# A hybrid SSD and gated-MLP layer: state products in three float32r parts, and the decay matrix made in place from rows loaded by direction

## The chip, the core and the metric

The kernel runs on one core of a Trainium2 chip, as one program in one launch. The metric is the device time of one execution in microseconds (us), first to last instruction plus what lies around them. TensorE is PE in the profile, VectorE DVE, ScalarE ACT, GpSimd POOL, and SyncE, which issues most loads, SP.

## What is computed

One layer of a trunk works on 256 latent tokens that read a prefix of 256 context tokens; the width is 2048. One input projection feeds a Mamba-2 state-space part (SSD; 32 heads of 64 in 8 groups, state size 128, two chunks of 128 tokens, both directions) and a gating MLP. All is float32. The part that matters here, for one direction:

```python
xbc = silu(dwconv_rows(z[..., :XBC_W], conv_w, conv_b))       # x, B and C of all groups
acs = cumsum(dt * A, axis=2)                                  # per chunk
decay_to_end = exp(a_tot[:, :, None] - acs)
states = einsum('bckgn,bckgr,bckgrp->bcgrpn', Bc, decay_to_end, xdt)
...
CB    = einsum('bcqgn,bckgn->bcgqk', Cc, Bc)
Lmat  = exp(where(mask, acs_t[..., :, None] - acs_t[..., None, :], -inf))
y_diag = einsum('bcgqk,bcgrqk,bckgrp->bcqgrp', CB, Lmat, xdt)
y_off  = einsum('bcqgn,bcgrpn,bcqgr->bcqgrp', Cc, h_starts, exp(acs))
y = y_diag + y_off                                            # then gates, norms, output projection
```

The context tokens only make the states from which the latent scans of both directions start.

## The kernel before, in words

**Projection.** The 4096 columns of x, B and C are done in 32 tiles of 128 columns. A group g has four: tiles 4g and 4g+1 (x), 4g+2 (B) and 4g+3 (C, latent tokens alone, so 256 wide in place of 512). A float32 product of nearly full precision is made of three products of float32r parts. ACT casts a weight half to its high part, DVE subtracts that from the raw half for the low part (`hi_w`, `lo_w`, lines 542 and 548, 128x1024 each), and `mm3` (lines 140 to 142) issues high by high, low by high and high by low for each of 16 pieces of the contraction. So a tile of 512 is 48 matmuls into one PSUM bank, `psx`; the tiles take turns between two such banks. Tiles 0 to 3, 12, 13 and 15 are made earlier; 12, 13 and 15 wait in SBUF (`y`, `zq`).

**After its products** a tile goes through ACT (line 607, middle tap and bias: `xbc<-psx,pc`), DVE (line 623, the other taps of the convolution, which read the PSUM bank as well: 8 instructions, 4 for a tile of 256) and ACT (line 626, silu). Its bank is free after the last tap. x and B are also turned to have tokens on partitions, by DVE and two DMAs (`tx`, `Dx`, `xk`; `tb`, `Db`, `bk`).

**The SSD of a group.** The names in the profile are: `xw` (POOL, line 785), x times dt times the decay to the end, for the states of the context; `psc`, the product of it with B over two tiles of context tokens (line 868, plain float32); `xl` and `psl`, the same for the latent tokens; `hs`, the states at the start of each chunk (ACT copies `psc`, POOL and DVE add the rest, lines 878 to 890); `pcb`, `cbb` and `cbf`, C by B and its two triangles; `M` (POOL line 896, DVE line 904), C by B times dt in both directions; `pso`, C by `hs` (plain float32); `psy`, the product of the decayed M with x; `yo`, `yc`, `yz` and `pty`, the outputs on their way into `y`.

**The decay matrix.** The cumulated logarithms lie in a DRAM scratch `acs`. For each group one POOL DMA copies its 2048 values to all partitions (`R`, 1 MB, line 724). ACT adds a column to each of its 16 blocks of 128x128 (line 820, `ssd_d`), DVE takes the minimum of the two directions into another tile `E` (line 827, two instructions), ACT takes the exponential of all of it (line 833), with a table load ahead of it and one behind it for the next silu, and DVE multiplies M into E (line 906). `R` has one buffer; the load for the next group waits for the second minimum.

**What sets the order.** Each engine runs its instructions in the order of the code. That order comes from a queue: `later(dt, fn)` puts a step at a due time on a clock that the loop over the projection's pieces drives, 1.3 for each two pieces (0.65 in a tile of 256), and `pump` issues what is due. `plan_tile` gives every step its offset from the end of its tile. `late` moves the whole second part of a group (from `ssd_cb` on), and `td` its end:

```python
for t, fn in [(6, ssd_cb), (6, ssd_states), ..., (12, ssd_o), ..., (16 + td, ssd_yd), (16.9 + td, ssd_yc), ...]:
    later(d0 + t, lambda fn=fn: fn(g))
plan_d(d0 + 11, g + 1, 1.5)      # the next group's decay matrix: four calls of ssd_d,
plan_e(d0 + 17, g + 1)           # then the minima and the exponential
```

`cv1`, `cv2` and `cv3` are pools of one, two and three buffers for each tag.

## Time and profile before

| what | value |
|---|---|
| median of three runs | 962.25 us (961.64 to 963.29) |
| the profiled execution | 962.39 us, its span 960.6 us, clock granted to PE 0.998 |
| busy in the span: PE, DVE, ACT, POOL | 950.8, 675.0, 481.8, 192.1 us |
| psc of a group (line 868), 8 groups | 4 records each, 15.3 us in all, 596 ns each |
| decay rows: blocks (820), minima (827), exponentials (833) | 128, 16 and 8 instructions |

Starts are in us from the start of the span. A plain float32 matmul leaves two records in the profile. Rows on PE overlap, since matmuls are pipelined: the time that one holds PE is the distance to the next start, not the length shown. DVE and ACT rows overlap by less than 0.1 us.

### The profile page before, as it was taken

To read this page: it belongs to the slowest core of one execution; us is meant where nothing else is said; L and a number is where in the kernel's file an instruction comes from. 1 tells how busy PE (TensorE), PEld (TensorE's weight loads), DVE (VectorE), ACT (ScalarE), POOL (GpSimd) and SP (SyncE) were. 2 spreads that over 40 slices of the span, in tenths; PEclk is the share of its full clock that TensorE was granted. 3 is DMA by queue.
4 is the path that set the end of the run, shared out by engine and by line. 5 is a ranking of instruction groups with operands and counts; after the bars stand their busy time and mean duration, and the time that the engine had idled before them with its cause. 6 is when DMAs were issued, how large, how long until landed. Compare 5 with 4: busy or idle time off the path is not lost.

```text
span 960.6 us, 13754 instructions
## 1 busy us (share of the span) xinstructions
PE 950.8 (99%) x5128; PEld 769.6 (80%) x5128; DVE 675.0 (70%) x1108; ACT 481.8 (50%) x728; POOL 192.1 (20%) x294
## 2 busy tenths in 40 slices
PE   9999999999999999999999999999999999999997
PEld 4688888778787878787888888888888888888885
DVE  6888899889787776676766776766666665445636
ACT  4344358565564544455445443455665554355522
POOL 0000002423424324243000000043445440000000
PEclk9999999999999999999999999999999999999999
DMA  9999967468668667467787777786666666556722
GB/s 366 418 415 416 365 232 203 124 167 190 168 148 224 146 205 160 143 180 258 296 304 283 261 275 294 269 304 215 220 219 211 228 211 215 186 190 243 267 88 87
DMA packets 149970, 225.63 MB, mean 235 GB/s; under 512 B 119296, under 2 KB 119552, under 8 KB 127248
## 3 DMA queue, kind: packets, MB, share of 16 engines
q1 hardware_dynamic: 142992, 207.08, 64.0%
q0 software_dynamic: 6336, 16.86, 5.3%
q8 instruction: 40, 0.66, 0.3%
q10 hardware_dynamic: 576, 0.82, 0.2%
q14 instruction: 26, 0.21, 0.1%
HBM read 211.29 MB, written 9.25 MB: 230 GB/s over the span
## 4 chain that ended last, share of the span: by engine, by line
PE 93%; DVE 3%; DMA 2%; issue 1%; POOL 1%; ACT 0%; SPq 0%; POOLq 0%; ACTq 0%
PE pa L1192 12%; PE pa L1191 12%; PE pa L1193 12%; PE psx L140 9%; PE psx L142 9%; PE psx L141 9%; PE pm L1232 3%; PE pm L1233 3%; PE pm L1234 3%; PE pq L1234 2%; PE pq L1232 2%; PE pq L1233 2%; PE psada L253 2%; DMA ada<-in_wada_dram 1%; PE pso L920 1%; PE psc L868 1%
## 5 line engine op out<-in xcount | busy, mean ns | idle before, releaser
L87 DVE TENSOR_TENSOR lo_w<-w,hi_w 128x1024 fp32r<-128x1024 f32 x173 | 209.8, 1221 | 133.8 <-ACT hi_w L86 133.7
L86 ACT CAST hi_w<-w 128x1024 fp32r<-128x1024 f32 x173 | 181.9, 1053 | 206.4 <-PE pa L1193 138.1
L1191 PE MATMUL pa<-hi_w,hhi 128*128 128x512 f32 x512 | 200.5, 392 | 0.0
L1193 PE MATMUL pa<-hi_w,hlo 128*128 128x512 f32 x512 | 199.3, 389 | 0.0
L1192 PE MATMUL pa<-lo_w,hhi 128*128 128x512 f32 x512 | 199.2, 389 | 0.0
L140 PE MATMUL psx<-hhi,hi_w 128*128 128x512 f32 (+1 forms) x400 | 151.3, 378 | 1.0 <-DVE xbc L623 1.0
L142 PE MATMUL psx<-hhi,lo_w 128*128 128x512 f32 (+1 forms) x400 | 145.6, 364 | 0.0
L141 PE MATMUL psx<-hlo,hi_w 128*128 128x512 f32 (+1 forms) x400 | 145.6, 364 | 0.0
L1191 PEld LDWEIGHTS pa<-hi_w,hhi 128*128 128x128 f32 x512 | 96.1, 188 | 20.2 <-issue 0.4
L1193 PEld LDWEIGHTS pa<-hi_w,hlo 128*128 128x128 f32 x512 | 96.1, 188 | 20.0
L1192 PEld LDWEIGHTS pa<-lo_w,hhi 128*128 128x128 f32 x512 | 96.1, 188 | 19.9 <-issue 0.2
L548 DVE TENSOR_TENSOR lo_w<-w,hi_w 128x1024 fp32r<-128x1024 f32 x61 | 76.9, 1268 | 17.1 <-ACT hi_w L542 17.0
L623 DVE SCALAR_TENSOR_TENSOR xbc<-psx,pc,xbc 128x248 f32<-128x248 f32 (+1 forms) x204 | 83.3, 471 | 7.7 <-ACT xbc L607 6.9
L140 PEld LDWEIGHTS psx<-hhi,hi_w 128*128 128x128 f32 x400 | 75.4, 189 | 15.5 <-issue 3.1
L141 PEld LDWEIGHTS psx<-hlo,hi_w 128*128 128x128 f32 x400 | 75.5, 189 | 13.0 <-issue 1.7
L542 ACT CAST hi_w<-w 128x1024 fp32r<-128x1024 f32 x61 | 63.4, 1043 | 44.6 <-PE psx L141 30.8
L142 PEld LDWEIGHTS psx<-hhi,lo_w 128*128 128x128 f32 x400 | 75.4, 189 | 12.2
L1232 PE MATMUL pm<-hi_w,hhi 128*128 128x512 f32 x128 | 49.8, 389 | 0.0
L1233 PE MATMUL pm<-lo_w,hhi 128*128 128x512 f32 x128 | 49.8, 389 | 0.0
L1234 PE MATMUL pm<-hi_w,hlo 128*128 128x512 f32 x128 | 49.8, 389 | 0.0
L1071 DVE SCALAR_TENSOR_TENSOR junk<-gate,cb 128x2048 bf16<-128x2048 f32 x16 | 36.6, 2291 | 18.4 <-DMA gate<-in_wada_dram 18.4
L1096 POOL DMA_DIRECT2D y<-T x64 | 36.9, 584 | 47.6 <-ACT sq L1167 32.6
(268 smaller groups left out, 1405.7 us busy)
## 6 DMA issues: line engine op xcount, KB each, us to landing
w<-in_wlat_dram SPq DMA_DIRECT2D x64, 1024.0 KB, 4.9
w<-in_wout_dram SPq DMA_DIRECT2D x32, 1024.0 KB, 4.8
w<-in_wxbc_dram SPq DMA_DIRECT2D x25, 1024.0 KB, 6.6
ada<-in_wada_dram SPq DMA_DIRECT2D x24, 1024.0 KB, 13.7
gate<-in_wada_dram SPq DMA_DIRECT2D x16, 1024.0 KB, 5.4
ada<-in_wada_dram SPq DMA_DIRECT2D x16, 512.0 KB, 12.4
R<-acs POOLq DMA_DIRECT2D x8, 1024.0 KB, 7.2
wst<-in_wst_dram SPq DMA_DIRECT2D x15, 480.0 KB, 12.9
```

The costliest lines, as they stand in the source:

```text
L86: nc.scalar.copy(hi, raw)
L87: nc.vector.tensor_tensor(lo, raw, hi.bitcast(F32), op=ALU.subtract)
L140: nc.tensor.matmul(ps, lhsT=whi, rhs=hhi[k][:, s], start=start, stop=False)
L141: nc.tensor.matmul(ps, lhsT=whi, rhs=hlo[k][:, s], start=False, stop=False)
L142: nc.tensor.matmul(ps, lhsT=wlo, rhs=hhi[k][:, s], start=False, stop=stop)
L623: nc.vector.scalar_tensor_tensor(ao, zi, cw[:, k : k + 1], ao, op0=ALU.mult, op1=ALU.add)
L1191: nc.tensor.matmul(pa[tk], lhsT=hhi[k][:, t], rhs=whi[:, w], start=k == 0, stop=False)
L1192: nc.tensor.matmul(pa[tk], lhsT=hhi[k][:, t], rhs=wlo[:, w], start=False, stop=False)
L1193: nc.tensor.matmul(pa[tk], lhsT=hlo[k][:, t], rhs=whi[:, w], start=False, stop=k == KT - 1)
L1232: nc.tensor.matmul(p, lhsT=yh[:, t], rhs=whi[:, w], start=j == 0, stop=False)
L1233: nc.tensor.matmul(p, lhsT=yh[:, t], rhs=wlo[:, w], start=False, stop=False)
L1234: nc.tensor.matmul(p, lhsT=yl[:, t], rhs=whi[:, w], start=False, stop=hf == 0 and j == 15)
```

## The change

**State products.** For groups 1 to 6 both operands of `psc` are split, as the weights are. `ssd_w` writes x's share for each of the two context tiles apart (`xr`, POOL). `ssd_wp` casts each to its high part (`xwh`, ACT, 128x512) and subtracts (`xwl`, DVE, 128x512); `ssd_bp` does so with B (`bp`, ACT and DVE, 128x256). `ssd_states` then issues three float32r matmuls for each tile, six for a group, in place of two plain ones. Groups 0 and 7 keep their plain products. `pso` stays as it was (`out_parts` is false for every group, so `ssd_cp` and `ssd_hp` are never called).

**Decay rows.** `R` becomes two tiles, `R1` and `R0`, one for each direction, each loaded on its own (512 KB). The minimum is written over `R0`, and exponential and M's product stay there, so there is no `E`. Hence `R1` of the next group waits for the minima of this one as before, but `R0` for `psy` of this group. ACT's blocks of `R1` keep their place (`d0 + 11`); those of `R0` move to `d0 + 24 + td`, 1.0 apart, and minima and exponential from `d0 + 17` to `d0 + 28.5 + td`.

**Places.** `late` is 18 in place of 14 for group 1 and 20 in place of 17 for group 3; some other steps of these groups move by 1.5 to 7.5.

```diff
-    acs = drp.tile([32, 4 * P], F32, name="acs")
+    acs = drp.tile([2, 32, 2 * P], F32, name="acs")
...
-    def row_load(g):
+    def row_load(g, d):
...
-        R = cv1.tile([P, 4, 2, 2, P], F32, tag="R", name=f"R{g}")
-        nc.gpsimd.dma_start(R.rearrange("p h d c q -> p (h d c q)"),
-                            acs[4 * g : 4 * g + 4, :].rearrange("h x -> (h x)").unsqueeze(0).partition_broadcast(P))
-        rows_[g] = R
+        R = cv1.tile([P, 4, 2, P], F32, tag=f"R{d}", name=f"R{d}_{g}")
+        nc.gpsimd.dma_start(R.rearrange("p h c q -> p (h c q)"),
+                            acs[d, 4 * g : 4 * g + 4, :].rearrange("h x -> (h x)").unsqueeze(0).partition_broadcast(P))
+        rows_[g, d] = R
...
+    def out_parts(g):
+        return False
+
+    def state_parts(g):
+        return 0 < g < NGRP - 1
...
+            if t is not None:
+                S["xr", t] = cv2.tile([P, 2, 256], F32, tag="tt", name=f"xr{g}{t}")
...
+    def hi_lo(hi, lo, raw):
+        nc.scalar.copy(hi, raw)
+        nc.vector.tensor_tensor(lo, raw, hi.bitcast(F32), op=ALU.subtract)
+
+    def pair4(g, nm):
+        return [cv1.tile([P, 2, 2, 256], F32R, tag=f"{w}p", name=f"{nm}{w}{g}") for w in "hl"]
+
+    def ssd_wp(g, t):
+        S = gs_[g]
+        if t == 0:
+            S["xp"] = pair4(g, "xw")
+        hi_lo(S["xp"][0][:, t], S["xp"][1][:, t], S["xr", t])
+
+    def ssd_bp(g):
+        S = gs_[g]
+        bp = S["bp"] = cv1.tile([P, 2, 2, P], F32R, tag="yo1", name=f"bp{g}")
+        hi_lo(bp[:, 0], bp[:, 1], S["bk"][:, 0:2])
...
     def ssd_min(g, c):
-        R = rows_[g]
-        if c == 0:
-            gs_.setdefault(g, {})["E"] = cv1.tile([P, 2, 4, P], F32, tag="E", name=f"E{g}")
-        nc.vector.tensor_tensor(gs_[g]["E"][:, c], R[:, :, 0, c, :], R[:, :, 1, c, :], op=ALU.min)
+        R = rows_[g, 0]
+        gs_.setdefault(g, {})["E"] = R
+        nc.vector.tensor_tensor(R[:, :, c, :], R[:, :, c, :], rows_[g, 1][:, :, c, :], op=ALU.min)
         if c == 1:
-            later(12 if g == 4 else 0, lambda: row_load(g + 1))
+            later(LATER_B.get(g, 0), lambda: row_load(g + 1, 1))
...
         for t in range(2):
-            nc.tensor.matmul(psc, lhsT=bk[:, t, :], rhs=xw[:, t], start=t == 0, stop=t == 1)
+            if state_parts(g):
+                bh, bl = (S["bp"][:, i, t] for i in range(2))
+                xh, xo = (p[:, t] for p in S["xp"])
+                nc.tensor.matmul(psc, lhsT=bh, rhs=xh, start=t == 0, stop=False)
+                nc.tensor.matmul(psc, lhsT=bh, rhs=xo, start=False, stop=False)
+                nc.tensor.matmul(psc, lhsT=bl, rhs=xh, start=False, stop=t == 1)
+            else:
+                nc.tensor.matmul(psc, lhsT=bk[:, t, :], rhs=S["xw"][:, t], start=t == 0, stop=t == 1)
...
-            late = max(late, 17.0 if i == 15 else 14.0)
+            late = max(late, {7: 18.0, 15: 20.0}.get(i, 14.0))
...
+            if state_parts(g):
+                WS = 1.5 * (g == 3)
+                for t in range(2):
+                    later(d0 + tx + tw + 1.3 * t + WS, lambda t=t: ssd_w(g, t))
+                    later(d0 + tx + tw + WP + 1.5 * t + WS, lambda t=t: ssd_wp(g, t))
+            else:
+                later(d0 + tx + tw, lambda: ssd_w(g))
...
+                later(d0 + tx + BP + 7.5 * (g == 3), lambda: ssd_bp(g))
...
+                          (16 + td, ssd_yd), (16.9 + td, ssd_yc), (17.2 + td, lambda g: row_load(g + 1, 0)),
...
-            plan_d(d0 + 11, g + 1, 1.5)
-            plan_e(d0 + 17, g + 1)
+            plan_d(d0 + 11, g + 1, 1.5, 1)
+            plan_d(d0 + 24 + td, g + 1, 1.0, 0)
+            plan_e(d0 + 28.5 + td, g + 1)
+
+    WP, BP, TP = 3.0, 14.5, 8.0
```

**What stands where, at group 1.** On PE, the products of group 1's second part stood right behind tile 9 and ahead of the first product of tile 10 (`psx10`) before:

```order
L142 MATMUL psx9_2049<-hhi15_131,lo_w11_1934 128x512
L851 MATMUL pcb1_2149<-xbc7_1911,xbc6_1830 128x128 x2
L868 MATMUL psc1_2152<-xw1_1981,bk1_1953 128x512 x2
L871 MATMUL psl1_2155<-xl1_2024,bk1_1953 128x256 x2
L140 MATMUL psx10_2158<-hhi0_116,hi_w12_1979 128x512
```

Now they stand behind 18 of the 48 products of tile 10:

```order
L142 MATMUL psx10_2155<-hhi5_121,lo_w12_1996 128x512
L890 MATMUL pcb1_2196<-xbc7_1913,xbc6_1832 128x128 x2
L910 MATMUL psc1_2199<-xwh1_2023,bp1_2140 128x512
L911 MATMUL psc1_2199<-xwl1_2024,bp1_2140 128x512
L912 MATMUL psc1_2199<-xwh1_2023,bp1_2140 128x512
L910 MATMUL psc1_2199<-xwh1_2023,bp1_2140 128x512
L911 MATMUL psc1_2199<-xwl1_2024,bp1_2140 128x512
L912 MATMUL psc1_2199<-xwh1_2023,bp1_2140 128x512
L917 MATMUL psl1_2206<-xl1_2075,bk1_1955 128x256 x2
L140 MATMUL psx10_2155<-hhi6_122,hi_w12_1981 128x512
```

Two plain products became six, and the whole block moved 18 matmuls back; the same holds for `pso1` behind it.

On ACT, the exponential of group 1's decay matrix (`E1`) stood between the copy of group 0's `psy` and the silu of tile 8:

```order
L954 COPY yc0_2079<-psy0_2060 128x512
L833 ACT_TABLE_LOAD
L833 ACTIVATE E1_2081<-E1_2081 128x1024
L626 ACT_TABLE_LOAD
L626 ACTIVATE xbc8_2056<-xbc8_2056 128x512
L542 CAST hi_w14_2122<-w7_1868 128x1024
L607 ACTIVATE xbc9_2165<-psx9_2049,pc_87 128x512
L542 CAST hi_w15_2167<-w7_1868 128x1024
L878 COPY hs1_2187<-psc1_2152 128x2x256
L820 ACTIVATE R2_2092<-R2_2092,y_68 128x128 x4
L626 ACTIVATE xbc9_2165<-xbc9_2165 128x512
L542 CAST hi_w16_2237<-w8_1977 128x1024
```

Now it stands one tile later, between tile 9's first pass over its bank and the copy of `psc1` to `hs1`, with the cast of B and the blocks of `R0` ahead of it:

```order
L542 CAST hi_w14_2119<-w7_1870 128x1024
L800 CAST bp1_2140<-bk1_1955 128x256
L858 ACTIVATE R0_1_2088<-R0_1_2088,y_68 128x128 x6
L607 ACTIVATE xbc9_2162<-psx9_2047,pc_87 128x512
L542 CAST hi_w15_2164<-w7_1870 128x1024
L858 ACTIVATE R0_1_2088<-R0_1_2088,y_68 128x128 x2
L870 ACT_TABLE_LOAD
L870 ACTIVATE R0_1_2088<-R0_1_2088 128x1024
L626 ACT_TABLE_LOAD
L626 ACTIVATE xbc9_2162<-xbc9_2162 128x512
L924 COPY hs1_2231<-psc1_2199 128x2x256
L542 CAST hi_w16_2235<-w8_1979 128x1024
```

The silu of tile 9, the copy to `hs1` and the cast of `hi_w16` now come behind the exponential of this group.

On DVE, behind the taps of the stored tile 12, the minima of group 2 stood ahead of the taps of tile 10, and M's products of group 1 had been issued before these rows:

```order
L623 SCALAR_TENSOR_TENSOR xbc12_2248<-y_68,pc_87,xbc12_2248 128x254
L738 STREAM_TRANSPOSE tx21_2266<-xbc9_2165 128x4x4x32
L926 TENSOR_TENSOR yo10_2270<-pso10_2231,ed_1460 128x512
L926 TENSOR_TENSOR yo11_2276<-pso11_2232,ed_1460 128x512
L738 STREAM_TRANSPOSE yc1_2307<-psy1_2298 128x4x4x32
L827 TENSOR_TENSOR E2_2311<-R2_2092 128x512 x2
L623 SCALAR_TENSOR_TENSOR xbc10_2320<-psx10_2158,pc_87,xbc10_2320 128x4x62
```

Now M's products of group 1 stand there, and the minima of group 2 are gone from this place:

```order
L623 SCALAR_TENSOR_TENSOR xbc12_2237<-y_68,pc_87,xbc12_2237 128x254
L950 SCALAR_TENSOR_TENSOR M10_2222<-cbf1_2217,dtt_1459,M10_2222 128x128 x4
L952 TENSOR_TENSOR R0_1_2088<-M10_2222,R0_1_2088 128x4x128
L746 STREAM_TRANSPOSE tx21_2264<-xbc9_2162 128x4x4x32
L950 SCALAR_TENSOR_TENSOR M11_2276<-cbf1_2217,dtt_1459,M11_2276 128x128 x4
L952 TENSOR_TENSOR R0_1_2088<-M11_2276,R0_1_2088 128x4x128
L980 TENSOR_TENSOR yo10_2312<-pso10_2284,ed_1460 128x512
L623 SCALAR_TENSOR_TENSOR xbc10_2302<-psx10_2155,pc_87,xbc10_2302 128x4x62
```

`M11` is one of two products that start on POOL and go through the single buffer of M, so it follows the DVE product of `M10`; `yo11` and `yc1` moved behind the taps of tile 10.

## The prediction

> **What bounds the kernel now.** I read the shares and the chain on the page first, then what PE waited for, then the stretch around the one wait that this change touches.

> ```profile
> PE 950.8 (99%) x5128; PEld 769.6 (80%) x5128; DVE 675.0 (70%) x1108; ACT 481.8 (50%) x728; POOL 192.1 (20%) x294
> ...
> PE 93%; DVE 3%; DMA 2%; issue 1%; POOL 1%; ACT 0%; SPq 0%; POOLq 0%; ACTq 0%
> ```

> PE is busy for 99% of the span and is 93% of the chain that ended last. So time comes from two places: work that PE need not do, and waits of PE. In the list of PE's waits two fall into the SSD:

> ```profile
> PE psx L140 <- DVE xbc L623: 1.0, 1, 1.0
> PE psc L868 <- POOL xw L785: 0.5, 1, 0.5
> ```

> The second is group 7's, which the change leaves alone. The first is tile 14's first product, which needs the bank whose last tap of tile 10 DVE had not done. The chain of waits leads there, at group 1's end:

> ```profile
> 208.99 3.14 DVE xbc L623 x8
> 212.12 0.62 DVE tx L738
> 212.74 1.17 DVE yo L926 x2
> 213.92 0.62 DVE yc L738
> 214.54 2.11 DVE E L827 x2
> 216.65 2.43 DVE xbc L623 x7
> 219.29 0.48 DVE xbc L623
> 219.90 0.47 PE psx L140
> ```

> DVE had no gap for 11 us; the minima of group 2 (2.11) stood ahead of the taps. PE, which waited 1.0, would have started at 218.9.

> **Part 1: the six products.** PE's timeline at group 1 (start, length, ..., shape, count):

> ```profile
> 194.69 0.39 PE L140 MATMUL psx<-hhi,hi_w 128*128 128x512 f32 x1
> ...
> 195.82 0.39 PE L142 MATMUL psx<-hhi,lo_w 128*128 128x512 f32 x1
> 196.05 0.60 PE L851 MATMUL pcb<-xbc,xbc 128*128 128x128 f32 x4
> 196.49 1.88 PE L868 MATMUL psc<-xw,bk 128*128 128x512 f32 x4
> 198.21 1.03 PE L871 MATMUL psl<-xl,bk 128*128 128x256 f32 x4
> ...
> 242.21 1.88 PE L868 MATMUL psc<-xw,bk 128*128 128x512 f32 x4
> ```

> The two plain products hold PE from 196.49 to 198.21, 1.72. Six float32r matmuls of the same width ran from 194.69 to 196.05, 1.36. That is 0.36 saved for a group and 2.16 for groups 1 to 6, all on the engine that bounds. The six from 194.69 also loaded a weight each at that pace, so I add nothing for weights.

> **Part 2: the casts and subtractions.** Each of six groups gets two ACT casts and two DVE subtractions of 128x512, and one of half that size on each. A copy of 128x512 is 0.59 on ACT (the row at 198.41 below), two operands of that size take DVE about 0.6 (188.76 to 189.36 below). So about 1.5 us more for each engine and group. ACT is half idle. On DVE, two subtractions of group 1 fall around 183 to 185.5, ahead of the taps of tile 8, which waited for PE then; they cost nothing there. If that cover were gone, 1.2 us would pass to the taps of tile 8.

> **Part 3: the decay matrix of group 1.** Here the change makes a new chain, which I walk through with durations of before. ACT, DVE and POOL in that stretch:

> ```profile
> 191.63 1.06 ACT L833 ACTIVATE E<-E 128x1024 f32<-128x1024 f32 x1 [3.68 <-DVE E L827]
> 192.71 1.28 ACT L626 ACT_TABLE_LOAD   x1
> 194.00 0.63 ACT L626 ACTIVATE xbc<-xbc 128x512 f32<-128x512 f32 x1
> 194.54 1.03 ACT L542 CAST hi_w<-w 128x1024 fp32r<-128x1024 f32 x1
> 196.25 0.78 ACT L607 ACTIVATE xbc<-psx,pc 128x512 f32<-128x512 f32 x1 [0.67 <-PE psx L142]
> 196.93 1.03 ACT L542 CAST hi_w<-w 128x1024 fp32r<-128x1024 f32 x1
> 198.41 0.59 ACT L878 COPY hs<-psc 128x512 f32<-128x512 f32 x1 [0.45 <-PE psc L868]
> 199.37 1.28 ACT L820 ACTIVATE R<-R,y 128x128 f32<-128x128 f32 x4 [0.38 <-DMA R<-acs]
> ```

> ```profile
> 188.76 0.68 DVE L827 TENSOR_TENSOR E<-R 128x512 f32<-128x512 f32 x1
> 189.36 1.63 DVE L548 TENSOR_TENSOR lo_w<-w,hi_w 128x1024 fp32r<-128x1024 f32 x1
> ...
> 198.02 3.17 DVE L623 SCALAR_TENSOR_TENSOR xbc<-psx,pc,xbc 128x248 f32<-128x248 f32 x8
> 201.11 1.21 DVE L548 TENSOR_TENSOR lo_w<-w,hi_w 128x1024 fp32r<-128x1024 f32 x1
> 202.24 0.75 DVE L890 TENSOR_TENSOR hs<-psl,hs 128x256 f32<-128x256 f32 x2
> 202.91 1.13 DVE L904 SCALAR_TENSOR_TENSOR M<-cbf,dtt,M 128x128 f32<-128x128 f32 x4
> ...
> 205.98 1.14 DVE L904 SCALAR_TENSOR_TENSOR M<-cbf,dtt,M 128x128 f32<-128x128 f32 x4 [1.22 <-POOL M L896]
> ...
> 207.77 1.22 DVE L548 TENSOR_TENSOR lo_w<-w,hi_w 128x1024 fp32r<-128x1024 f32 x1
> ```

> Group 0 keeps its places on PE, so ACT's first pass over tile 9 starts at 196.25 as before and ends near 197.0. From there one thing follows the other in the new order. DVE: taps of tile 9, 3.09 (198.02 to 201.11), to 200.1; `lo_w15`, 1.13, to 201.3; two minima, 1.2, to 202.5. ACT: exponential 1.08, table 1.29, silu of tile 9 0.54 (191.63, 192.71, 194.00, 194.54), to 205.4; the copy to `hs1`, 0.6, to 206.0; `hi_w16`, 1.0, to 207.0. DVE again: `lo_w16`, 1.13; two additions to `hs1`, 0.67, to 208.8; taps of the stored tile 12, 3.14, to 211.9; then M's products: from the first of them to the second 3.07 (202.91 to 205.98, POOL's M between), and 1.79 to what follows (207.77), to 216.8. `tx21` hides in the time of POOL's M. Then one `yo`, 0.6, and the eight taps of tile 10, 3.14, to 220.5, and 0.1 to PE. Tile 14 starts at 220.6, where it started at 219.90 before and could start at 218.9 less the 0.36 saved. So group 1 gains nothing and loses 0.7: PE waits 2.1 there in place of 1.0. `psy1`, which needs the second product with M (216.8), will show part of that wait, near 1; the rest is at tile 14. The minima of group 2 did leave this place, but 2.1 us of them are less than the M products, the table loads and the exponential that came into it.

> **Part 4: the loads.** A load of 1 MB becomes two of 512 KB, 16 in all, and `acs` is stored by two DMAs. What counts is `R0` of group 1: it now waits for `psy0` and stands behind work on POOL.

> ```profile
> 178.22 2.74 POOL L785 TENSOR_TENSOR xw<-xk,ed 128x256 f32<-128x256 f32 x4 [2.82 <-DMA xk<-Dx]
> ...
> 181.91 1.23 POOL L792 TENSOR_TENSOR xl<-xk,ed 128x256 f32<-128x256 f32 x2
> 185.23 3.07 POOL L934 TENSOR_TENSOR y<-y,yo 128x256 f32<-128x256 f32 x4 [2.08 <-DVE yo L926]
> ```

> ```profile
> DMA to landing us min/median/max: 4.8/7.2/8.3
> ...
> y<-T POOLq DMA_DIRECT2D x64, 32.0 KB, 3.6
> ```

> (The first line is that of `R`'s eight loads.) POOL's M of group 0 now stands behind two products of x in place of four, 1.4 earlier; DVE's subtraction takes 0.6 of it back, so the additions of `yo` start near 184.4 and end at 187.5; `xl1` adds 1.2: the load is issued at 188.7. ACT must have done six blocks (0.3 each) before 196.25, so it must land by 194.3, within 5.6. No row shows 512 KB on this queue. The bounds are 3.6 (32 KB) and 8.3 (the slowest MB); half the bytes lie halfway between 3.6 and the median 7.2, so I take 5.4: on time by 0.2. Each 0.1 beyond 5.6 goes into the chain of part 3 whole, and waits behind it on ACT are the pass over tile 9 and `hi_w15`. [...]

> For group 2 the same steps, from an issue at 222.7 (behind the additions of `yo11`), leave `bp2` some 2 us ahead of its product, which starts 0.7 later than 242.21. In groups 3 to 6 `R0` is needed later after its issue, and I cost it nothing; the cover is ACT's idle half.

> **Sum.** 962.39 (the profiled execution) + 0.7 (group 1, its own 0.36 included) − 5 × 0.36 (groups 2 to 6) = 961.3. The median lies 0.14 lower: **961.1 us**, 0.12% less than 962.25. I count within 0.2% (1.92 us) as no change, which is about what a measurement of this kernel can tell apart: below 960.33 is faster, above 964.17 slower.

> **Rivals.**
> - *The wait at group 1 does not grow.* Sixteen steps of 0.1 less would take back 1.6 of the 2.1. For it: some steps carry lengths from stretches in which POOL was at work, and the last taps of tile 10 ran at 0.35 each (2.43 for seven) where I count 0.39. Against it: the lengths are those of quiet stretches too. With the old wait the time is 962.25 − 2.16 = 960.1; with none, 959.1. Faster. It decides if the chain is 0.8 or more shorter than I make it.
> - *The 512 KB loads take as long as 1 MB.* For it: 1 MB and 32 KB differ by a factor of two alone, so a fixed part is most of it. Against it: half the bytes. At 7.2 the chain is 1.6 later: 962.7, no change. At 8.3 it is 2.7 later, and `psc2` waits a further 0.9 for `bp2`, since group 2 has 2 to spare: 964.7, slower. It is slower from a landing of about 8.0 in both groups.
> - *DVE's pairs are stretched by POOL.* The minima show the spread:

> ```profile
> L827 DVE TENSOR_TENSOR E<-R x16: 649/682/1223, 156.0 to 410.2; 128x512 f32<-128x512 f32 x16
> ```

>   At worst a subtraction of two SBUF operands takes 0.54 more. In the chain of part 3, `lo_w16` runs while POOL adds to `hs1`; one or two such stretches make 0.5 to 1.1: 961.6 to 962.2, no change. [...]
> - *The parts save nothing on PE*, if switching between plain float32 and float32r costs some 0.06 for each matmul: 962.25 + 1.05 = 963.3. Against it, the row at 196.05 follows a float32r matmul at the common pace.

> **Chances.** My forecast (960.4 to 962.0) 0.40; the wait does not grow 0.33; loads late by less than the slower point 0.11, beyond it 0.08; stretched pairs 0.06; nothing saved 0.02. So faster 0.33, no change 0.59, slower 0.08. The range is 959.3 (the wait nearly gone) to 963.3 (a load of 7.8, or nothing saved); the likeliest case alone has 960.4 to 962.0.

> **What would show it.** `psc` of groups 1 to 6 as six rows 0.23 apart. Waits of PE: `psy1` on DVE's product with M, near 1, and tile 14 on the taps, near 1. DVE's taps of tile 10 ending at 220.5; if they end before 219.7, the first rival holds. ACT idle ahead of `R0`'s blocks on the DMA tells the second, and the landing of 16 loads settles it. I am wrong most of all if a step of the chain in part 3 does not wait for the one ahead of it, or if another group has a chain like it that I did not see.

## The result, and the profile after

The changed kernel takes 973.61 us (median of four runs, 973.18 to 974.26), the kernel before 961.94 beside it (961.60 to 963.29): a ratio of 1.0119, 95% interval 1.0102 to 1.0137, or 11.7 us slower. The prediction had 961.1. The profiled execution of after took 973.91 us, its span 972.2. The page's first rows and its chain:

```profile
PE 952.6 (98%) x5140; PEld 773.3 (80%) x5140; DVE 693.0 (71%) x1126; ACT 490.2 (50%) x746; POOL 200.0 (21%) x303
...
PE 80%; DMA 7%; DVE 7%; issue 2%; POOL 2%; ACT 1%; SPq 0%; POOLq 0%; DVEq 0%; ACTq 0%
```

PE was 93% of the chain and is 80%; transfers and DVE have 14% of it between them. PE's waits (us in total, times, longest) say where:

```profile
PE psc L910 <- ACT bp L800: 5.6, 2, 4.6
PE pso L974 <- DVE hs L936: 1.8, 2, 1.0
...
PE psy L1000 <- DVE R L952: 1.4, 1, 1.4
...
PE pa L1262 <- DVE lo_w L87: 1.0, 1, 1.0
PE psx L140 <- DVE xbc L623: 0.8, 1, 0.8
```

`psy` and `psx` (1.4 and 0.8) are the wait of group 1 that was forecast at 2.1. The largest, 4.6, was not forecast. It is group 2's. PE's timeline there, and behind it windows of the same stretch (columns: us, then busy time and count of PE, PEld, DVE, ACT, POOL, then the granted clock, DMA share and GB/s):

```profile
242.65 0.60 PE L890 MATMUL pcb<-xbc,xbc 128*128 128x128 f32 x4
247.84 0.80 PE L910 MATMUL psc<-xwh,bp 128*128 128x512 f32 x1 [4.58 <-ACT bp L800]
248.43 0.63 PE L911 MATMUL psc<-xwl,bp 128*128 128x512 f32 x1
248.86 0.63 PE L912 MATMUL psc<-xwh,bp 128*128 128x512 f32 x1
...
250.56 1.91 PE L917 MATMUL psl<-xl,bk 128*128 128x256 f32 x4
259.54 1.88 PE L974 MATMUL pso<-hs,xbc 128*128 128x512 f32 x4
```

```profile
243.00:246.00 3.00, 0.26 (x3) 0.06 (x1) 3.00 (x9) 2.80 (x4) 0.59 (x1) 1.00 0.57 223
246.00:247.00 1.00, 0.00 (x0) 0.00 (x0) 1.00 (x2) 1.00 (x2) 0.00 (x0) 0.66 0.16 61
247.00:249.00 2.00, 1.16 (x3) 0.97 (x4) 1.74 (x3) 2.00 (x5) 0.00 (x0) 0.50 0.44 82
...
253.00:254.00 1.00, 1.00 (x5) 0.76 (x5) 1.00 (x4) 0.00 (x0) 1.00 (x2) 0.93 0.59 90
```

PE stood still from 243.26 to 247.84. While it did, its granted clock fell from 1.00 to 0.50, and stayed there until about 253: the products that came at last are 0.43 apart in place of 0.23. From `pcb` to `pso` of this group are 16.89 us (242.65 to 259.54) where before has 9.84 (241.76 to 251.60). So group 2 alone lost 7.05.

Set against before by the starts of `pcb` and `psy`, the changed kernel is 0.15 ahead at `psy` of group 0 and 0.89 behind at `pcb` of group 2. It is 8.88 behind at `pcb` of group 4 (the 7.05 of group 2 and a wait of 0.8 at `pso` of group 3 are in it), 11.15 at `psy` of group 4 (`psc` and `pso` of it waited 1.0 each), 9.90 at `psy` of group 7, and 11.6 at the end. In groups 5 and 6 the change gains 0.3 each, as was meant. The 0.6 gained in group 7 is not from the products, which are plain there: before waits 0.5 for `xw` in that group, and the kernel without any parts, below, gains the 0.6 too. Behind the SSD the changed kernel loses 1.6 again, 1.0 of that in the one wait for `lo_w` (`pa` above).

### The profile page after: what moved, and what is told of

Its sections match the earlier page's. It is cut to its first block, busy times and chain, and to the rows that moved or that the text cites. A ratio compares the mean times of both kernels' runs of the same rounds, so it can differ in the third digit from the quotient of the medians.

```text
span 972.2 us, 13844 instructions
## 1 busy us (share of the span) xinstructions
PE 952.6 (98%) x5140; PEld 773.3 (80%) x5140; DVE 693.0 (71%) x1126; ACT 490.2 (50%) x746; POOL 200.0 (21%) x303
## 4 chain that ended last, share of the span: by engine, by line
PE 80%; DMA 7%; DVE 7%; issue 2%; POOL 2%; ACT 1%; SPq 0%; POOLq 0%; DVEq 0%; ACTq 0%
PE pa L1261 12%; PE pa L1262 12%; PE pa L1263 12%; PE psx L140 6%; PE psx L142 6%; PE psx L141 6%; PE pm L1304 3%; PE pm L1302 3%; PE pm L1303 3%; DMA ada<-in_wada_dram 3%; DVE xbc L623 2%; PE pq L1304 2%; PE pq L1303 2%; PE pq L1302 2%; PE psada L253 2%
## 5 line engine op out<-in xcount | busy, mean ns | idle before, releaser
L87 DVE TENSOR_TENSOR lo_w<-w,hi_w 128x1024 fp32r<-128x1024 f32 x173 | 209.9, 1221 | 131.3 <-ACT hi_w L86 131.2
L140 PE MATMUL psx<-hhi,hi_w 128*128 128x512 f32 (+1 forms) x400 | 151.8, 379 | 0.8 <-DVE xbc L623 0.8
L142 PE MATMUL psx<-hhi,lo_w 128*128 128x512 f32 (+1 forms) x400 | 145.7, 364 | 0.0
L623 DVE SCALAR_TENSOR_TENSOR xbc<-psx,pc,xbc 128x248 f32<-128x248 f32 (+1 forms) x204 | 83.2, 470 | 10.1 <-ACT xbc L607 9.4
L548 DVE TENSOR_TENSOR lo_w<-w,hi_w 128x1024 fp32r<-128x1024 f32 x61 | 81.7, 1347 | 9.0 <-ACT hi_w L542 8.9
L140 PEld LDWEIGHTS psx<-hhi,hi_w 128*128 128x128 f32 x400 | 75.6, 189 | 15.5 <-issue 4.0
L142 PEld LDWEIGHTS psx<-hhi,lo_w 128*128 128x128 f32 x400 | 75.6, 189 | 12.4
L542 ACT CAST hi_w<-w 128x1024 fp32r<-128x1024 f32 x61 | 63.4, 1043 | 38.1 <-PE psx L141 28.7
L858 ACT ACTIVATE R<-R,y 128x128 f32<-128x128 f32 x128 | 41.4, 391 | 15.3 <-DMA R<-acs 15.3
```

The source lines that it names most:

```text
L87: nc.vector.tensor_tensor(lo, raw, hi.bitcast(F32), op=ALU.subtract)
L140: nc.tensor.matmul(ps, lhsT=whi, rhs=hhi[k][:, s], start=start, stop=False)
L142: nc.tensor.matmul(ps, lhsT=wlo, rhs=hhi[k][:, s], start=False, stop=stop)
L623: nc.vector.scalar_tensor_tensor(ao, zi, cw[:, k : k + 1], ao, op0=ALU.mult, op1=ALU.add)
```

## Experiments: which part of the change

**The decay matrix alone.** Here and below, each median stands against that of the kernel before run beside it (961.7 to 962.0).

```diff
     def state_parts(g):
-        return 0 < g < NGRP - 1
+        return False
```

> The changed kernel with plain state products in every group (state_parts false): no casts, no subtractions; the decay matrix in place, its loads and the places stay as changed. Theory A (the loss comes from the parts: casts of x stand in ACT's queue behind POOL and a DRAM store, and the cast of B behind the exponential): only group 1's later chain stays, 963 to 965 us, and no wait of PE at psc of group 2. Theory B (the late R0 load and the in-place decay matrix make the loss by themselves): 970 or more, with group 2's exponential still at about 242.

970.81 us (969.75 to 974.22), ratio 1.0100 (1.0076 to 1.0123), 9.1 slower. So the parts are not the main cause, and the theory that they were is refuted; most of the loss comes without them. `psc` of group 2 waited here too, 2.1, but for `bk`, the loaded B itself. The other theory has the time right, but not its sign: the exponential of group 2 came at 238.16 and not near 242.

**The six products alone.** Before, with six float32r products of other operands written to `psc`. It leaves out the states of groups 1 to 6: x and B of the context are not read there, so that nothing has to be made for the products and they wait for nothing.

```diff
-            nc.tensor.matmul(psc, lhsT=bk[:, t, :], rhs=xw[:, t], start=t == 0, stop=t == 1)
+            if 0 < g < NGRP - 1:      # three float32r products of hhi and hlo for each t
+                ...
+            else:
+                nc.tensor.matmul(psc, lhsT=bk[:, t, :], rhs=xw[:, t], start=t == 0, stop=t == 1)
```

> The kernel before, in which psc of groups 1 to 6 is made by six float32r products of the projection's own input parts in place of the two plain products (x's and B's context parts are not read by it, so these states do not enter the result). No casts, no subtractions, all else as before. My first term: six groups by 0.36 = 2.16 less, 959.6. If the products saved nothing: 961.7.

960.31 us (959.85 to 960.75), ratio 0.9982 (0.9973 to 0.9992): 1.4 faster. Its timeline at group 2:

```profile
241.40 0.60 PE L851 MATMUL pcb<-xbc,xbc 128*128 128x128 f32 x4
241.76 1.62 PE L870 MATMUL psc<-hlo,hhi 128*128 128x512 f32 x6
243.22 1.02 PE L875 MATMUL psl<-xl,bk 128*128 128x256 f32 x4
```

`pcb` to `psl` is 1.82 where it was 2.16, so 0.34 a group. From `psy` of group 0 to that of group 7 this kernel needs 251.52 us where before needs 253.75, 2.2 less. The span of this execution is 1.95 shorter than that of before, and the medians are 1.4 apart. In the changed kernel the parts cost 2.8 over the decay matrix alone (973.6 against 970.8), though their products save 1.4. So what makes the parts costs 4.2.

## Experiments: what holds group 2

**PE kept busy.** After, with 20 products of no use ahead of `psc` of group 2.

```diff
+        if g == 2:
+            for n in range(20):
+                nc.tensor.matmul(psc, lhsT=hhi[0][:, 0:P], rhs=hhi[0], start=True, stop=True)
```

> The changed kernel with 20 float32r matmuls of 128x512 that nobody reads, issued on PE right ahead of group 2's state products (4.6 us of work in the wait of 4.6 us). Theory of the clock (PE's clock halves in a wait of over 3 us and stays at half for some 5 us of the work behind it): the rows of psc in group 2 are 0.23 apart in place of 0.43, and the time falls by 2.6 to 971.0 although PE does more. Rival (the slow rows come from the parts' operands or the weights just written): time the same or longer, 973.6 to 974.5.

974.24 us, ratio 1.0131 (1.0116 to 1.0146): no gain, where the theory of the clock had 971.0. The clock stayed whole (0.999 in the mean of the span) and the rows ran at full pace (0.23 to 0.24 apart from the second on), as that theory has it:

```profile
243.07 4.79 PE L908 MATMUL psc<-hhi 128*128 128x512 f32 x20
248.07 0.50 PE L913 MATMUL psc<-xwh,bp 128*128 128x512 f32 x1 [0.21 <-ACT bp L800]
```

But `psy` of group 2 came only 1.0 earlier (265.81 against 266.83), with a wait for `hs` ahead of it. So the halved clock is worth 1 us at most: the work behind it on DVE would not have been ready either.

**B cast earlier.** After, with ACT's and DVE's splitting of B of group 2 five steps of the clock earlier.

```diff
-                later(d0 + tx + BP + 7.5 * (g == 3), lambda: ssd_bp(g))
+                later(d0 + tx + BP + 7.5 * (g == 3) - 5 * (g == 2), lambda: ssd_bp(g))
```

> The changed kernel with the cast and subtraction of B of group 2 five steps of the queue's clock earlier: on ACT ahead of the table load of group 2's exponential, on DVE right behind the minima. Theory C (the place of this cast in ACT's queue is the whole cause): the wait at psc goes and with it the low clock, 966 to 967. Theory A with a backlog (DVE runs without a gap from 237 to 262, since the taps of tile 13 came late): the wait moves to pso of group 2, which needs hs2 from DVE near 257.5 and wants it at 252: 972 to 974.

973.97 us, ratio 1.0127 (1.0112 to 1.0142). `psc` no longer waited, and the wait came back, as long as it had been, one step on:

```profile
243.35 0.48 PE L910 MATMUL psc<-xwh,bp 128*128 128x512 f32 x1
...
258.11 3.75 PE L974 MATMUL pso<-hs,xbc 128*128 128x512 f32 x4 [4.60 <-DVE hs L936]
```

So `bp` was only the first of PE's wants to come late. DVE was behind.

**Group 2 later on PE.** After, with the second part of group 2 two steps of the clock later.

```diff
-            late = max(late, {7: 18.0, 15: 20.0}.get(i, 14.0))
+            late = max(late, {7: 18.0, 11: 16.0, 15: 20.0}.get(i, 14.0))
```

> The changed kernel, with the second part of group 2 moved back on PE by two steps of the clock (late 16 in place of 14), about 2 us; nothing else. Theory A (the 4.6 us wait of group 2's products with B, and the halved clock behind it, are a matter of where PE stands when the chain of tile 9, xr, xwl, taps and decay rows on DVE, ACT and POOL ends): the wait falls from 4.6 to about 2.5, the clock is not halved, and some 4 of the 7 us of group 2 come back: 968 to 971. Theory B (DVE is full from 237 to 262 and sets the end whatever PE does meanwhile, as the two runs with dummy matmuls and with the earlier cast had it): the wait goes to hs or to tile 14 or 16, and the time stays at 973 to 975.

971.55 us (970.49 to 972.01), ratio 1.0100 (1.0086 to 1.0114), 2 of the 12 back. Between the theories: the wait moved to a tile's first product (`psx` for DVE's taps, 2.9 at 245.74), the clock was halved behind it (246.26 to 249.67), and `psc` started at 248.70, later than the 247.84 of after.

**A place of its own for `xr`.** The trace of after shows why DVE is behind. The chain of group 2, in order of time (start, us, what):

```profile
224.76 6.29 DMA Dx<-tx
...
231.22 1.19 POOL xr L797 x2
...
233.86 2.11 POOL xr L797 x2
236.65 1.00 DVE xwl L801
237.65 3.14 DVE xbc L623 x7
...
242.71 2.40 DVE xbc L623 x7
...
246.45 1.03 ACT hi_w L542
247.48 0.32 ACT bp L800
```

`xr` shares two buffers (the tag `tt`) with the transposes `tx`, so the first `xr` waits until a transpose has been stored to DRAM, 6.29 us, and the second until DVE has split the first. DVE ran in the order of the code: behind the second `xwl` (236.65) came the taps of tile 13 (237.65), the minima (241.51) and the taps of tile 14 (242.71). ACT's cast of B (247.48) came behind the silu that waited for the last of those taps (245.91). DVE was busy 5.17 of the 10 us from 230 to 240, where before has 9.43; from there it had hardly a gap until 260 (busy 9.74 and 9.69 of the next two 10 us).

The store itself is that long beside `R0`'s load, which was issued at 224.67, 0.09 ahead of it. After, then the kernel with `R0` in two buffers of the next section, which has no load there (transfers on the way from 222 to 226: KB, us from issue to landing):

```profile
R<-acs POOLq DMA_DIRECT2D x1, 512.0 KB, 6.1
...
Dx<-tx SPq DMA_DIRECT2D x1, 256.0 KB, 6.3
```

```profile
Dx<-tx SPq DMA_DIRECT2D x1, 256.0 KB, 3.4
```

In all seven kernels in which `R0`'s load goes out right ahead of this store it took 6.0 to 6.5, in the nine others 3.0 to 3.6. So the late load of `R0` and the shared buffer make this chain together. No run has the parts without that load beside the store, so their shares are not shown.

The run here takes away the buffer: it writes `xr` into the low part's own tile. It leaves out the low part of x's share, since `xr` is a float32r tile there; the steps stay the same.

```diff
-                S["xr", t] = cv2.tile([P, 2, 256], F32, tag="tt", name=f"xr{g}{t}")
+                if t == 0:
+                    S["xp"] = pair4(g, "xw")
+                S["xr", t] = S["xp"][1][:, t]
```

> The changed kernel, with x's share for a context tile (xr) written by POOL into the tile that later holds its low part, in place of the buffers of the transposes (tag tt); POOL rounds it to float32r there, so the low part holds nothing that counts. All instructions and their places stay. Theory A: xr of group 2 no longer waits for the store of tile 12's transpose, so it starts near 225.5 in place of 231.2, the taps of tile 13 and 14 end 2 to 3 us sooner, bp2 is ready near 245, PE waits 2 at psc in place of 4.6 and its clock stays full: about 968 (966 to 970). Theory B: no change, 973 to 974.

969.90 us (969.21 to 972.28), ratio 1.0090 (1.0075 to 1.0105): 3.7 faster than after, close to the 4.2 that making the parts costs. In its profiled execution (972.28, the slowest) the mean clock of the span is 0.999, and `psc` waits 1.4 at most. So the shared buffers are where the parts lose most.

**Both repairs**, the last two together:

> The changed kernel with both repairs: xr written into the low part's own tile (the run that gave 969.9, x's share rounded to float32r there before it is split) and group 2's second part two steps later. If what is left after the first is PE's place in group 2 (1.4 of wait at psc, 2.8 at three products with hs), 967 to 969. If it is DVE's backlog, 969 to 971. Neither theory expects it below the kernel before, 961.7, since the late exponential alone had cost 4.9.

971.72 us (968.46 to 972.61), ratio 1.0095 (1.0082 to 1.0109): no better than the place alone, and in neither of the expected ranges. In its profiled execution, the fastest (968.46), PE's largest wait was `pso` for `hs`, 2.7. So it is not shown that PE's place in group 2 is what is left, and not that DVE's backlog is.

## Experiments: what the decay matrix costs

Here all products are plain, and the change is built up from the kernel before.

**Places.** Before, with `late` of 18 and 20 and two steps of group 1 later, as in after.

```diff
-            late = max(late, 17.0 if i == 15 else 14.0)
+            late = max(late, {7: 18.0, 15: 20.0}.get(i, 14.0))
...
-            later(d0 + tx + tw + (3 if late_w else 0), lambda: ssd_wl(g))
+            later(d0 + tx + tw + (3 if late_w else 0) + 3 * (g == 1), lambda: ssd_wl(g))
```

> The kernel before, with the changed places of groups 1 and 3 (late 18 and 20, xl and the skip product of group 1 by 3 later); rows, E, the exponential's place and the plain products as before. Theory D (the exponential's late place makes the loss of the decay part): 961.5 to 963.5. Theory E (group 1's later places alone push POOL's and SP's queues, so that B of group 2 comes late): 966 or more, with PE waiting at psc of group 2.

962.99 us (962.78 to 963.77), ratio 1.0012 (1.0003 to 1.0021): 1.3 slower.

**Minima and exponential late**, as well, and the load of group 5's rows at once behind the minima, as in after:

```diff
-            later(12 if g == 4 else 0, lambda: row_load(g + 1))
+            later(0, lambda: row_load(g + 1))
...
-            plan_e(d0 + 17, g + 1)
+            plan_e(d0 + 28.5 + td, g + 1)
```

> As the run with the places alone, and the minima and the exponential moved to d0 + 28.5 + td; one load of 1 MB for a group, behind the minima at once in every group, and E apart. Theory D: the loss of the decay part appears here, 967 to 971, since tile 9's silu, hs1 and hi_w16 wait for the exponential. Theory F (R0's load, which must wait for psy, makes it): 962 to 964 here.

966.62 us (966.08 to 969.06), ratio 1.0053 (1.0039 to 1.0067): 4.9 slower. `psy` waited 2.0 in two groups for its decayed M. This is the chain of part 3 of the prediction, without the parts, the new loads and the new tiles.

**Each load in two**, as well (`h` is the first of two heads):

```diff
-        nc.gpsimd.dma_start(R.rearrange("p h d c q -> p (h d c q)"), acs[4 * g : 4 * g + 4, :]...)
+        for h in (0, 2):
+            nc.gpsimd.dma_start(R[:, h : h + 2]..., acs[4 * g + h : 4 * g + h + 2, :]...)
```

> The kernel before with the new places and the late minima and exponential (the run that gave 966.6), and each load of 1 MB of decay rows cut in two of 512 KB, two heads each, one behind the other, into the same tile. Theory C (the step from 966.6 to 969.7 is the splitting of the loads into smaller pieces, which slows the other transfers around them, bk2 above all, so that psc of group 2 waits): bk2 lands near 245.5, psc of group 2 waits about 2 with rows of double length, and the time is 968.5 to 970. Theory D (it is the blocks of R0 made late and in place): 966 to 967.2, no wait of psc of group 2.

965.66 us (965.38 to 966.20), ratio 1.0042 (1.0028 to 1.0055): 3.9 slower, and no wait at `psc` of group 2. More and smaller loads cost nothing that shows.

**One load for each direction**, in place of one for two heads: the scratch as in after, `[2, 32, 2 * P]`, and stored by two DMAs; `R` one tile still, with the directions one behind the other in it, the minimum still to `E`.

```diff
-        for h in (0, 2):
-            ...
+        for d in (1, 0):
+            nc.gpsimd.dma_start(R[:, d]..., acs[d, 4 * g : 4 * g + 4, :]...)
```

> The run with two loads of two heads each (965.7), with the scratch laid out by direction and one load for each direction, as in the changed kernel; R stays one tile with one buffer, the minimum goes to E, plain products, blocks of rows on ACT where the kernel before has them. Theory F (the layout by direction in DRAM is what slows the transfers around it): bk2 lands near 245.5, psc of group 2 waits about 2, 968 to 970. Theory G (the layout does not matter; it is the tiles R1 and R0 in place of R and E, where they lie or what their loads wait for): 965 to 966.5, no wait at psc of group 2.

968.39 us (967.28 to 969.35), ratio 1.0066 (1.0053 to 1.0078): 6.4 slower, 2.5 more than the run above, though the loads carry the same bytes in pieces of the same 4 KB. In the profiled run 2.0 is lost ahead of group 0 (a wait of 1.3 at `psx`; `psy` of group 0 stands 2.0 later than in the run above), and 1.7 more up to `psy` of group 2, whose `psc` waited 1.4 for `bk`. The next kernel has the same scratch and loses nothing ahead of group 0, so that part is not the layout as such.

**Tiles of their own**, `R1` with one buffer and `R0` with two, the minimum in place:

```diff
-        R = cv1.tile([P, 2, 4, 2, P], F32, tag="R", name=f"R{g}")
+        R = (cv1 if d else cv2).tile([P, 4, 2, P], F32, tag=f"R{d}", name=f"R{d}_{g}")
```

> The run with R0 in two buffers and both loads behind the minima (969.7), with one change: the blocks of R0 go back on ACT to the place that those of R1 have (d0 + 11, 1.5 apart), as in the kernel before; plain float32 products, the new places, minima and exponential late. The loads by direction and the minimum written in place stay. Theory D (ACT's late blocks of R0 are what the run with R0 in two buffers costs over the 965.7 of the run with two loads of two heads each): 965.5 to 967, and no wait of psc of group 2 for bk. Theory E (it is how the loads by direction meet the other transfers: the layout of the scratch, or where the tiles lie): bk2 lands near 245.5 again, psc of group 2 waits about 2 at half the clock, 969 to 970.

968.69 us (967.31 to 973.78), ratio 1.0072 (1.0058 to 1.0087): 6.9 slower; the 0.5 more than with one tile is within the spread. `psc` of group 2 waited 2.0 for `bk`.

**Its two loads swapped** (`R0` first):

> The run with R0 in two buffers, its blocks at the early place (968.7) and the two loads of a group in the other order, R0 ahead of R1; nothing else. If the lateness of bk2 in group 2 is a matter of which transfers meet by chance at one moment, the swap may move it: 965.5 to 969, and the landing of bk2 differs. If it belongs to the layout or the tiles, 968 to 970 with the same wait of 2 at psc of group 2.

967.92 us (967.53 to 968.13), ratio 1.0059 (1.0045 to 1.0072): 5.9 slower. `psc` of group 2 did not wait for `bk` now, and 1.0 came back at most, which the spread of the run above (967.31 to 973.78) does not tell from nothing. The swap also parted the two loads in time. `R0`, with a buffer free, no longer stood on POOL behind `R1`'s wait for the minima: it was issued at 232.56 in place of 236.62. So one load of rows stood beside `bk` in place of two, and the last of `bk` took 4.0 us in place of 8.4.

**The blocks of `R0` late**, unswapped (`plan_d(d0 + 24 + td, ...)` for `R0`):

> The changed kernel with plain products (as the decay-only run), and R0 in two buffers, both directions loaded behind the minima, so that no load waits for psy; exponential and blocks in their late places. Theory D: 969 to 971, as the decay-only run (970.8). Theory F: 963 to 965.

969.68 us (968.99 to 971.24), ratio 1.0082 (1.0068 to 1.0096): 7.9 slower. One buffer for `R0`, which is the decay matrix of after, was 9.1.

How the loads by direction do harm shows in group 2. The run with loads by heads, then this one: SP's issue of B's loads, PE's `psc`, and of the transfers issued from 236.3 to 243 the weights' and the last of the four of `bk` (KB, us from issue to landing):

```profile
234.68 2.08 SPq L747 DMA_DIRECT2D bk<-Db  x4
243.26 1.88 PE L869 MATMUL psc<-xw,bk 128*128 128x512 f32 x4
w<-in_wxbc_dram SPq DMA_DIRECT2D x1, 1024.0 KB, 8.1
...
bk<-Db SPq DMA_DIRECT2D x1, 64.0 KB, 5.3
```

```profile
234.73 2.08 SPq L754 DMA_DIRECT2D bk<-Db  x4
245.57 3.50 PE L914 MATMUL psc<-xw,bk 128*128 128x512 f32 x4 [2.13 <-DMA bk<-Db]
w<-in_wxbc_dram SPq DMA_DIRECT2D x1, 1024.0 KB, 10.9
...
bk<-Db SPq DMA_DIRECT2D x1, 64.0 KB, 9.1
```

B's loads were issued at the same time (0.05 apart); in the second run the last of them took 9.1 in place of 5.3, too late for PE, and the weights beside it 10.9 in place of 8.1. The run with one tile, which differs from the first in the layout alone, has 8.4 and 11.5. Why one layout of the scratch meets the others worse stays open. It is not a dearer load as such: over the whole program the rows' queue holds 5.6% of the DMA engines with loads by heads and 5.7% by direction. That the wait went when one load of rows stood beside `bk` in place of two speaks for a matter of which transfers meet, but two loads by heads did no such harm, and the runs don't show what tells the two apart.

## Why the prediction was wrong

By its own steps:

- **Part 1, the products: right.** 0.36 forecast, 0.34 in the run with them alone, and the same in groups 5 and 6 of after, where nothing waits (`pcb` at 358.74 to `psl` at 360.56, 1.82 against 2.16). It asked for six rows 0.23 apart:

```profile
358.74 0.60 PE L890 MATMUL pcb<-xbc,xbc 128*128 128x128 f32 x4
...
359.42 0.40 PE L911 MATMUL psc<-xwl,bp 128*128 128x512 f32 x1
359.65 0.39 PE L912 MATMUL psc<-xwh,bp 128*128 128x512 f32 x1
...
360.56 1.02 PE L917 MATMUL psl<-xl,bk 128*128 128x256 f32 x4
```

  The size is in part luck. From the first of the six to `psl` are 1.46 us in the run with them alone (241.76 to 243.22) and not the 1.36 of the sum, and `pcb` ahead of them held PE 0.36 where it had 0.45 ahead of a plain product (241.76 to 242.21 before). At the end 1.4 of the 2.16 arrived.

- **Part 3, group 1: right.** The chain ran step by step as written: minima at 201.24, exponential 202.48, `hs1` 205.47, taps of the stored tile 12 at 208.96, and at its end:

```profile
216.26 0.69 DVE R L952
216.95 0.60 DVE yo L980
217.55 2.40 DVE xbc L623 x7
...
220.18 0.47 DVE xbc L623
```

  Taps done at 220.65 (forecast 220.5), tile 14 at 220.80 (220.6), PE's waits 1.4 + 0.8 (2.1). The rival that the wait does not grow fell here.

- **Part 4, the loads of `R0`: their length was right, and so was group 1.** The load was issued at 188.21 (forecast 188.7) and its blocks began at 192.54. All 16:

```profile
R<-acs POOLq DMA_DIRECT2D x16, 512.0 KB, 5.2
```

  5.2 for the forecast 5.4, and 4.3 for this one, so the rival of loads as slow as 1 MB fell. That halfway between two bounds came out so near is in part luck: the two kinds of 256 KB loads on the same queue in before took 6.8 and 7.5.

- **Part 4, groups 2 to 6: the step that failed.** It said that the same steps "leave `bp2` some 2 us ahead of its product", and that `R0` of groups 3 to 6 costs nothing. I followed one input of group 2, the load of `R0` from an issue at 222.7 (it was 224.67), and not what it runs beside, nor what stands ahead of `bp2` in the queues of DVE and ACT: `tx`'s store (6.3 beside that load, 3.4 without it), `xr` in the shared buffers, `xwl`, two tiles' taps, the minima. `bp2` came 4.6 late in place of 2 early. The runs put the size at 3.7 for the buffers. And without any parts the same group still lost, because `bk` landed late: SP issued it at 237.89 in the kernel with the decay matrix alone, behind that same store, where the kernel with loads by heads has 234.68, and beside `R1`'s load its last part took 6.7. Waits in groups 3 and 4, 1.0 each at most, were costed at nothing as well.

- **Part 2, casts and subtractions: under-sized, and wrongly covered.** I costed two subtractions of 0.6 and a half one, 1.5 a group. They took 0.77 and 0.41 in the mean, 11.7 us in all where 9 was said:

```profile
L801 DVE TENSOR_TENSOR xwl<-xr,xwh 128x512 fp32r<-128x512 f32 x12 | 9.2, 770 | 13.4 <-ACT xwh L800 13.2
...
L797 POOL TENSOR_TENSOR xr<-xk,ed 128x256 f32<-128x256 f32 x24 | 20.2, 863 | 30.9 <-DMA xk<-Dx 16.5 <-DVE xwl L801 7.5 <-DMA Dx<-tx 6.0
```

  The length is the lesser miss. I named what hides the work of group 1 and not what it waits for in the others: the second row has POOL waiting 7.5 for the subtraction and 6.0 for the transposes' store, and the first has DVE idle 13.4 ahead of them. I had read the buffer's tag in the diff and put no price on it.

- **The late minima.** Part 3 costed them at group 1 alone: a loss of 0.7 with the saved 0.36 in it, so 1.06. The run with late minima stands 0.86 behind the run with places alone at `psy` of group 2 (259.86 against 259.00), which agrees. But it stands 1.88 behind at `psy` of group 4 (321.53 against 319.65) and 2.8 at the end of the span (964.4 against 961.6). So as much again was lost in groups 3 and 4, where the prediction had nothing, and 1.0 more behind the SSD.

- **The rivals.** Stretched pairs held, and by more than their price. Of the twelve subtractions of 128x512 the six beside work of POOL took 0.86 in the mean, the others 0.68; of the minima the five beside work of POOL took 1.09, the others 0.68. The mean of `lo_w` of line 548 went from 1.268 to 1.347 us, 4.8 over 61 instructions, and two of them, of 4.50 and 3.60, make more than that:

```profile
284.63 3.60 DVE L548 TENSOR_TENSOR lo_w<-w,hi_w 128x1024 fp32r<-128x1024 f32 x1
```

  POOL worked without a break until 287.14 there (273.55 for the other), and both ended 1.09 behind its work. The rival had 0.54 as the worst. In the four kernels with parts in which this `lo_w` took 3.6, `pso` of group 3 waited 0.8; in the two with group 2 later, where it took 1.95, it did not. These rows show POOL's work and DVE's long rows at one time, and not what joins them: of the 21 `lo_w` of line 548 beside work of POOL in after, 11 took no more than 1.22, as most of the others did. Nothing saved fell with part 1. None of the rivals had a wait in group 2 of more than 0.9. The chance of 0.08 for slower rested on the length of `R0`'s load; the load did harm, but by what ran beside it.

The ladder of the decay matrix, in us over before: places 1.3, late minima 4.9, two loads 3.9, by direction 6.4, own tiles 6.9, late blocks 7.9, one buffer 9.1; the parts on top make 11.7. No step of it is the whole. Each has an interval of 0.9 to 2.3 us to either side, so of neighbours only places and late minima are clearly apart, and two loads and by direction barely. What stays open is why the loads by direction slow the transfers around them, and where the 1.6 behind the SSD goes beyond one wait of 1.0: that stage (end of the span less the start of `psy` of group 7) took 522.0 us before and 522.0 to 525.3 in the other kernels, 527.0 in the one profiled run that lay 5 us above its kernel's median. It grows with the waits of `pa` for `lo_w`: they are 2.5 where it took 525.3, and 3.9 where it took 527.0.

No version here that makes the parts beats the kernel before. The 960.3 of the products alone is about the most that they can bring in the order of before, with all that makes them free.

## What to carry to other kernels

Where a change has the same steps in each of several groups, follow the chain in each group whose neighbours differ, and for each new tile ask what was in its buffer before: here a shared buffer put a store to DRAM, stretched from 3.4 to 6.3 us by a load issued beside it, ahead of work that was costed at its own 1.5. When PE's wait is removed and comes back elsewhere at the same length (4.6 at `psc`, then 4.6 at `pso`), the bound is a queue that is behind, and its first idle gap, here DVE's ahead of `xwl`, is the place to mend. A saving on the engine that bounds is little beside one late chain: 0.34 for each of six groups against 7.05 in one.

## What was not expected of the hardware

```profile
245.00:246.00 1.00, 0.43 (x1) 0.30 (x2) 1.00 (x4) 0.00 (x0) 0.97 (x1) 0.92 1.02 257
246.00:247.00 1.00, 1.00 (x2) 0.34 (x1) 1.00 (x4) 0.00 (x0) 0.06 (x1) 0.50 0.63 134
...
249.00:250.00 1.00, 1.00 (x6) 0.85 (x5) 0.50 (x1) 0.89 (x3) 0.23 (x1) 0.88 1.38 190
```

In the run with both repairs a stop of 2.7 left it at 1.00:

```profile
255.00:256.00 1.00, 0.00 (x0) 0.00 (x0) 0.33 (x1) 0.90 (x4) 1.00 (x3) 1.00 0.39 61
```

What tells the two apart is where the stop lies on a grid of 3.413 us. In the traces of before and after the times between changes of the granted clock are whole multiples of that: in before it was whole for 952.32, 279 of them; in after it was whole for 242.35 ahead of the stop, half for 6.83 and whole for 716.80 behind it, 71, 2 and 210. With `R0` in two buffers the half clock lasted 3.41 (the shares 0.92 and 0.88 above put it from 245.83 to 249.25), with group 2 later as long (246.26 to 249.67), in the decay matrix alone 3.4 (a mean of 0.83 from 240 to 250), and with B cast earlier 6.8 (255.96 to 262.80).

In every step of these traces in which PE, at whole clock, stood for 1.96 us or more in all, the clock was halved at its end: 2.3 and 2.8 at the ends of before and after, 3.06 in after's stop, 2.9 with group 2 later, 2.5 with B cast earlier, 2.13 with `R0` in two buffers, 2.07 in the decay matrix alone, and least, 1.96, ahead of `psc` of group 2 with tiles of their own, where `psc` then took 3.55 in place of 1.88. In none with 1.72 or less was it halved: 1.48 at the end of after, and 1.72 in the run with both repairs (from 958.69 to 962.10, a wait of 1.48 and the 0.24 behind PE's last matmul). The stop of 2.1 lay within one step (242.42 to 245.83). The stop of 2.7 (254.07 to 256.81) was parted at 255.54, 1.5 and 1.3. The mean clock of that run agrees: on the steps from 255.54 the clock is halved at 965.51, 1.2 ahead of the end of the span (966.7), which makes 0.999. Where the limit lies between 1.72 and 1.96 is not shown.
